# Conditioning products of the first layer: VectorE sums beside the projections, or one-column TensorE products between attention units

## The chip, the cores and the metric

The kernel runs on one NeuronCore of a Trainium2 chip. The metric is the device time of one execution in microseconds (us); the kernel before takes 2411.71 us, the median of three runs (2411.21 to 2413.84).

## The reference

A two-layer encoder on one sequence of 1024 tokens with 1024 features. Each layer has a token mixer and a gated feed-forward network, and both are steered by a conditioning vector c. What the change touches is the first line of the loop, for layer 0:

```python
cond = jax.nn.silu(c)
for i in range(DEPTH):
    mod = (cond @ ada_w[i] + ada_b[i])[:, None, :]        # 1024 x 6144 matrix per layer
    sh1, sc1, g1, sh2, sc2, g2 = jnp.split(mod, 6, axis=-1)   # chunks 0 to 5
    h = rmsnorm(x, norm_mix[i]) * (1 + sc1) + sh1
    y = windowed_gqa(...) if i % 2 == 0 else dilated_attention(...)
    x = x + g1 * y
    h = rmsnorm(x, norm_ffn[i]) * (1 + sc2) + sh2
    x = x + g2 * swiglu(h, ffn_w_in[i], ffn_w_out[i])
return rmsnorm(x, final_norm)
```

The product `cond @ ada_w[i]` is a vector times a matrix: six chunks of 1024 columns, 4 MB of weights each. Chunks 2 to 5 of layer 0 are the gate of its attention, the shift and scale of its feed-forward network, and that network's gate. Layer 0 has windowed attention with 16 query heads and 4 key heads over 8 blocks of 128 queries.

## The kernel before

Activations lie feature-major: 8 groups of 128 features on the partitions, 1024 tokens in two halves of 512 along the free dimension. A projection is a sum over 8 groups; since each float32 operand is split into a high and a low fp32r part, one step of it is three TensorE matmuls (L284, L285, L286 in `acc3`). Weights come by DMA into `raw`, ScalarE writes the high part (L180) and GpSimd the low part (L181).

`start` normalises the first token half and runs six projections; `layer_a` then runs, in its block around `pre_w`, four query tiles, the value tiles (`v_tile`, 256 columns, weights `wv`) and the key tiles of the second half. Beside these it makes chunks 2, 3 and 4 of the conditioning: `ada_steps` loads 128x1024 pieces of the matrix (L148) and adds each, times its element of `cond`, into `ada_acc` on VectorE (L151 for the first, L153 for the other seven); `ada_end` sums `ada_acc` over partitions by eight one-column products with a column of ones (L167), adds the bias (L169) and, for the scale chunk, makes the gain. `step` issues two such steps after each projection tile, held back by `issue_after`.

Then come the 32 attention units: for one key head and one query block, `first` makes the scores of four query heads (L490, L491), VectorE adds the bias and takes the minimum (L493), ScalarE the exponential (L503), VectorE scales (L510); `second`, two units later, transposes the probabilities on TensorE (L532), splits them (L534 on ScalarE, L535 on VectorE) and multiplies by the values (L526). `weave` interleaves the two with projection steps of the list `fill` (query tiles of the second half, then the output projection of the first half, then the first feed-forward tile). Those take PSUM banks from `bank`, two of them (tag `d`) during the units.

Chunk 5 is made by the same VectorE steps, issued at the end of `layer_a` (the last line before `return EARLY_A`), and the six chunks of layer 1 follow during the feed-forward network of layer 0 (`self.bg`). There the sum over partitions takes a VectorE transpose and reduction (L124, L126) and four small matmuls (L131).

The Tile framework orders each engine's instructions by its own model of their times with the order of the program as priority; the order is fixed when the kernel is built, and each engine works through its queue in that order. All DMAs are issued from SP's queue.

Of the kernel before, what the change touches and what calls it, by code (L numbers as in the profile page):

```python
# [7 lines left out]
F = mybir.dt.float32  # L8
# [3 lines left out]
ALU = mybir.AluOpType  # L12
AX = mybir.AxisListType

P = 128
D = 1024
KT = D // P
T = 1024
HT = 512
# [10 lines left out]
V_NM, V_NF, V_FN, V_C, V_AB = 0, 16, 32, 40, 48  # L30
# [1 line left out]
N_FIRST = 6  # L32
ADA_LATE = 1
BIAS_DVE = 5
PRE_PE = True
PRE_BUFS = 4, 1
PRE = (2,) * 14
PRE_LAG = 4
N_DVE = 5
A_BUFS = 2  # L40
RAW1 = 3
# [29 lines left out]
def run(steps):  # L71
    for _ in steps:
        pass


class Trunk:
    def __init__(self, ctx, tc, a, out, layers=(0, 1)):
        self.tc, self.nc, self.a, self.out, self.layers = tc, tc.nc, a, out, layers
        self.ctx = ctx
        self.t2, self.sq = 3, ("t2", 3)  # L80
        self.plan, self.ready = deque(), deque()
        self.ada_pe = False

    def sb(self, name):
        return self.tc.tile_pool(name=name, bufs=1, reuse_waits="tile")
# [49 lines left out]
    def ada_gain(self, layer, j, k0, k1):  # L135
        off = (V_NF if j else V_NM) + 8 * layer
        self.nc.vector.scalar_tensor_tensor(self.gain[:, layer, j, k0:k1], self.mod[:, layer, 24 * j + 8 + k0:24 * j + 8 + k1], 1.0,
                                            self.vec[:, off + k0:off + k1], op0=ALU.add, op1=ALU.mult)

    def ada_steps(self, layer, chunks, pool, bufs=2, abufs=1):  # L140

        nc = self.nc
        rest = iter(())
        for c in chunks:
            acc = pool.tile([P, D], F, name="ada_acc", tag="ada_acc", bufs=abufs)
            for k in range(KT):
                w = pool.tile([P, D], F, name="ada_w", tag="ada_w", bufs=bufs)
                nc.sync.dma_start(w, self.a["ada_w"][layer, k * P:(k + 1) * P, c * D:(c + 1) * D])  # L148
                s = self.cond[:, k:k + 1]
                if k == 0:  # L150
                    nc.vector.tensor_scalar(acc, w, s, None, op0=ALU.mult)  # L151
                else:
                    nc.vector.scalar_tensor_tensor(acc, w, s, acc, op0=ALU.mult, op1=ALU.add)  # L153
                if k == ADA_LATE:
                    run(rest)
                yield
            rest = self.ada_end(layer, c, acc, pool, bufs)
            next(rest)
            yield
        run(rest)  # L160

    def ada_end(self, layer, c, acc, pool, bufs):
        if self.ada_pe:
            yield
            ps = self.norm_bank()
            for j in range(KT):
                self.nc.tensor.matmul(ps[:, j:j + 1], lhsT=acc[:, j * P:(j + 1) * P], rhs=self.ones[:, 0:1], start=True, stop=True)  # L167
            cols = slice(8 * c, 8 * c + 8)
            self.nc.vector.tensor_tensor(self.mod[:, layer, cols], ps[:, 0:KT], self.vec[:, V_AB + 48 * layer:V_AB + 48 * layer + 48][:, cols], op=ALU.add)  # L169
            if c in (1, 4):  # L170
                self.ada_gain(layer, c // 3, 0, KT)
            return
        tr = pool.tile([P, D], F, name="ada_t", tag="ada_w", bufs=bufs)
        yield from self.ada_columns(layer, acc, tr, pool, slice(8 * c, 8 * c + 8))
        if c in (1, 4):
            self.ada_gain(layer, c // 3, 0, KT)
# [528 lines left out]
    def layer_a(self, h, x_src):  # L705
        nc, a, sb = self.nc, self.a, self.sb
        self.t2, self.sq = 4, ("t2", 4)
        layer = 0
# [22 lines left out]
            yield from self.project_steps(ps, self.weight("a_w_q", p, g), h[t])  # L731
            self.q_out_a(p, g, t, ps)

        with self.raw2_es, sb("pre_w") as prew, sb("pre") as pre:
            self.norm_bank = lambda: psp.tile([P, HT], F, name="ps_n", tag="o", bufs=2)
            self.banks += [(psp, tag, 2) for tag in BANKS_A]
            bg = self.ada_steps(0, (2, 3, 4), pre, *PRE_BUFS)
            self.ada_pe = PRE_PE
            w = prew.tile([P, 3, KT, 256], R, name="wv")[:, 0:2]

            todo = deque(PRE)

            done = []

            def step():
                done.append(self.evac)
                with ExitStack() as s:
                    if len(done) > PRE_LAG:
                        s.enter_context(self.tc.issue_after(done[-1 - PRE_LAG]))
                    for _ in range(todo.popleft()):  # L750
                        next(bg, None)

            for g in range(4):
                if 2 + 4 + g >= N_FIRST:
                    run(q_tile(1, g, 0))
                    step()
            for i in range(2):
                self.load_w(a["a_w_v"][i], w[:, :, 4 * i:4 * i + 4].rearrange("p s k f -> p s (k f)"))
            for tb in range(4):
                v_tile([w], tb)  # L760
                step()
            for tb in range(4, 8):
                v_tile([w], tb)
                step()
            for j in range(2):
                k_tile(j, 1)
                step()
            run(bg)
        self.ada_pe = False
        self.banks = deque([(self.psn, "d", 2)])  # L770
        self.norm_bank = self.bank
        wp, wk = (es.enter_context(sb(n)) for n in ("probs_a", "work_a"))
# [40 lines left out]
        oTs = []  # L813
        self.fill_start([q_tile(p, g, 1) for p in range(2) for g in range(4)] + [out_0(d) for d in range(KT)] + [self.up_early(layer, spill)], FILL_A, LOOK_A, 64)
        units = [(t, hd, b) for t in range(2) for hd in range(4) for b in range(4 * t, 4 * t + 4)]
        pend = deque()
        for i, (t, hd, b) in enumerate(units):
            if i % 16 == 0:
                oTs.append([[self.htile([4, HT]) for _ in range(2)] for _ in range(2)])
            if i == 18:  # L820
                self.most = 1000
            if i in (16, 24):
                self.fill_until(32 * (i // 8 - 1))
            if b % 4 == 0:
                bias = self.bias_tiles(wp, dist, SLOPE_A[4 * hd:4 * hd + 4], 6, nc.vector if i < BIAS_DVE else None)
            pt = self.weave(i, first(hd, b, bias), second(*pend.popleft()) if len(pend) > 1 else None)
            pend.append((hd, b, pt, oTs[t]))
        while self.fill:
            self.fill_step()
        while pend:  # L830
# [18 lines left out]
        self.hf[1] = self.norm_half(self.xs[1], ssq, layer, 1, self.pool, lows=LOWS["a_half1"])  # L849
        for f in range(1, EARLY_A):  # L850
            self.up(f, (0,))
        run(self.ada_steps(0, (5,), self.paux))
        return EARLY_A


# [428 lines left out]
def _arrays(np, i):  # L1284

    c = np.ascontiguousarray

    def cols(w, idx):

        w = w[:, idx]  # L1290
        return c(w.reshape(KT, P, -1, P).transpose(2, 1, 0, 3)).reshape(-1, P, D)

    def per_part(v):
        return v.reshape(-1, P).T

    o = {}
    o["x"] = c(i["x"][0].T).reshape(KT, P, T)
    o["vec"] = c(np.concatenate([per_part(i["norm_mix"]), per_part(i["norm_ffn"]), per_part(i["final_norm"]),
                                 per_part(i["c"]), per_part(i["ada_b"])], axis=1))
    o["sink"] = c(i["a_sink"])  # L1300
    o["cst"], o["dist"] = _constants(np)
    o["ada_w"] = c(i["ada_w"])
    w = i["ada_w"][0][:, :2 * D].reshape(KT, P, 2, KT, P)
    for d0, n in FIRST_D:
        o[f"ada_w0_{d0}"] = c(w[:, :, :, d0:d0 + n].transpose(1, 0, 2, 3, 4)).reshape(P, 2 * D * n)
    w = i["ffn_w_in"].reshape(2, KT, P, 2, NF, P)
    o["ffn_w_in"] = c(w.transpose(0, 4, 3, 2, 1, 5)).reshape(2, NF, 2, P, D)
    o["ffn_w_out"] = c(i["ffn_w_out"])
    w = i["a_w_in"][0]
    e = np.arange(64)  # L1310
    pair = [np.concatenate([((2 * p + par) * 4 + g) * 64 + e for par in range(2)]) for p in range(2) for g in range(4)]
    o["a_w_q"] = cols(w, np.concatenate(pair)).reshape(2, 4, P, D)
    o["a_w_k"] = cols(w, 1024 + np.arange(256))
    o["a_w_first"] = c(w[:, np.concatenate(pair[:2] + [1024 + np.arange(256)] + pair[2:N_FIRST - 2])]).reshape(KT, P, N_FIRST * P)
    o["a_w_v"] = c(w[:, 1280:].reshape(2, 4, P, 256).transpose(0, 2, 1, 3)).reshape(2, P, D)
    o["a_w_out"] = cols(i["a_w_out"][0][np.concatenate(pair)], np.arange(D))
    w = i["b_w_in"][0]
    o["b_w_q"] = cols(w, np.concatenate([gi * 512 + kv * 256 + g * 64 + e for gi in range(3) for g in range(4) for kv in range(2)])).reshape(3, 4, P, D)
    o["b_w_k"] = cols(w, 1536 + np.arange(384))
    o["b_w_v"] = c(w[:, 1920:].reshape(4, 2, P, 384).transpose(0, 2, 1, 3)).reshape(4, P, 768)  # L1320
    rows = np.concatenate([kv * 256 + g * 64 + e for g in range(4) for kv in range(2)])
    w = i["b_w_out"][0][rows].reshape(4, P, 4, 2, P)
    o["b_w_out"] = c(w.transpose(2, 1, 3, 0, 4)).reshape(4, P, D)
    return o
# [20 lines left out]
```

## Time and profile before

| | |
|---|---|
| median of the runs | 2411.71 us |
| profiled execution | 2411.33 us |
| its span, first to last instruction | 2409.5 us |
| TensorE busy | 2256.8 us, 94% |
| VectorE busy | 1282.8 us, 53% |
| ScalarE busy | 881.3 us, 37% |
| GpSimd busy | 751.4 us, 31% |
| DMA | 248.83 MB, 103 GB/s mean |

Busy time is the union of the instructions' recorded spans. The ends of matmuls are modelled, so a busy TensorE isn't one at its peak; the distance from one start to the next tells what a matmul takes. Where a matmul is float32 by float32, as L167, L226 and L532 are, what the trace records is passes: the 24 products of L167 stand as 48 records. The granted clock is a share of 2.4 GHz.

### The profile page before, as it was taken

Reading aid. Unit: us, or ns where it says so; the run is one execution under the profiler, and the core shown is the slowest. Engines: PE = TensorE matmul, PEld = TensorE weight load, DVE = VectorE, ACT = ScalarE, POOL = GpSimd, SP = SyncE. Lnnn points to the kernel's source line nnn. Section 1 sums busy time; section 2 is a strip of 40 time slices with the busy share of each in tenths; the row PEclk is TensorE's granted clock in tenths of the full one; section 3 lists DMA queues with packets and bytes.
Section 4 is the critical chain, followed back from the end, with each engine's and each line's share of the span. In section 5 each row is a group of like instructions: output and inputs, shape, how many; then the busy total and the mean of one; then the engine's idle time right before and its main releaser. Section 6 shows DMA issues by size and latency. Waiting matters only on the chain.

```text
span 2409.5 us, 28051 instructions
## 1 busy us (share of the span) xinstructions
PE 2256.8 (94%) x10484; PEld 1863.5 (77%) x10484; DVE 1282.8 (53%) x2265; ACT 881.3 (37%) x1749; POOL 751.4 (31%) x483
## 2 busy tenths in 40 slices
PE   6799898988999999999989999797999999999997
PEld 5687676767788888888879878576788888888886
DVE  8869999578533333333362577786633332222325
ACT  4549887332111111111242788673411111111111
POOL 4525453453122122222233344344431212222210
PEclk9899998999999999999999999898999999999998
DMA  7441123666411111111234765736321111111101
GB/s 281 150 144 36 40 84 132 214 205 219 158 60 39 50 44 53 44 53 44 79 121 155 197 189 179 212 89 202 96 70 53 51 46 53 53 53 44 53 18 70
DMA packets 131224, 248.83 MB, mean 103 GB/s; under 512 B 39312, under 2 KB 66576, under 8 KB 130064
## 3 DMA queue, kind: packets, MB, share of 16 engines
q1 hardware_dynamic: 131088, 247.05, 32.1%
q8 instruction: 82, 1.34, 0.2%
q14 instruction: 54, 0.44, 0.1%
HBM read 214.20 MB, written 30.70 MB: 102 GB/s over the span
## 4 chain that ended last, share of the span: by engine, by line
PE 71%; DVE 16%; DMA 6%; issue 3%; ACT 3%; POOL 1%; SPq 1%; DVEq 0%; ACTq 0%; POOLq 0%
PE ps_d L284 22%; PE ps_d L285 22%; PE ps_d L286 22%; DMA ada_w<-in_ada_w 3%; DVE ada_acc L153 3%; DVE p L493 2%; DVE pp L535 2%; PE ps_o L526 1%; PE ps_t L532 1%; DVE ht L256 1%; DVE p L510 1%; DVE h L262 1%; DMA ml_all<-sd 1%; PE ps_s L491 1%; PE ps_s L490 1%
## 5 line engine op out<-in xcount | busy, mean ns | idle before, releaser
L284 PE MATMUL ps_d<-h,w 128*128 128x512 f32 x1968 | 780.8, 399 | 22.4 <-ACT w L180 11.1
L285 PE MATMUL ps_d<-h,w 128*128 128x512 f32 x1968 | 779.2, 396 | 11.4 <-DVE h L262 9.9
L286 PE MATMUL ps_d<-h,w 128*128 128x512 f32 x1968 | 775.9, 395 | 3.8 <-POOL w L181 3.8
L181 POOL TENSOR_TENSOR w<-raw,w 128x1024 fp32r<-128x1024 f32 (+1 forms) x178 | 431.2, 2424 | 758.7 <-ACT w L180 745.9
L284 PEld LDWEIGHTS ps_d<-h,w 128*128 128x128 f32 x1968 | 374.8, 191 | 96.3 <-ACT w L180 13.7
L285 PEld LDWEIGHTS ps_d<-h,w 128*128 128x128 f32 x1968 | 376.6, 191 | 84.3 <-DVE h L262 12.8
L286 PEld LDWEIGHTS ps_d<-h,w 128*128 128x128 f32 x1968 | 375.3, 191 | 84.7 <-POOL w L181 5.8
L401 DVE TENSOR_TENSOR u<-silu,ps_d 128x512 f32<-128x512 f32 x88 | 60.4, 686 | 607.6 <-PE ps_d L286 591.1
L354 DVE SCALAR_TENSOR_TENSOR x<-ps_d,mod,x 128x512 f32<-128x512 f32 x368 | 270.3, 747 | 149.2 <-PE ps_d L286 149.2
L180 ACT ACTIVATE w<-raw 128x1024 fp32r<-128x1024 f32 (+1 forms) x178 | 185.6, 1046 | 361.2 <-PE ps_d L286 295.3
L284 PE MATMUL ps_d<-act,wo 128*128 128x512 f32 x704 | 275.4, 391 | 8.9 <-DVE x L354 4.8
L286 PE MATMUL ps_d<-act,wo 128*128 128x512 f32 x704 | 274.3, 390 | 0.0
L285 PE MATMUL ps_d<-act,wo 128*128 128x512 f32 x704 | 274.2, 390 | 0.0
L181 POOL TENSOR_TENSOR wo<-raw,wo 128x1024 fp32r<-128x1024 f32 x44 | 105.6, 2399 | 432.7 <-ACT wo L180 425.3
L180 ACT ACTIVATE wo<-raw 128x1024 fp32r<-128x1024 f32 x44 | 46.7, 1060 | 382.8 <-PE ps_d L286 340.2
L284 PEld LDWEIGHTS ps_d<-act,wo 128*128 128x128 f32 x704 | 132.2, 188 | 39.0 <-DVE x L354 6.6
L286 PEld LDWEIGHTS ps_d<-act,wo 128*128 128x128 f32 x704 | 132.2, 188 | 27.5
L285 PEld LDWEIGHTS ps_d<-act,wo 128*128 128x128 f32 x704 | 132.3, 188 | 26.9
L403 DVE TENSOR_TENSOR act<-u,act 128x512 fp32r<-128x512 f32 x88 | 124.8, 1418 | 47.3 <-ACT act L402 47.1
L153 DVE SCALAR_TENSOR_TENSOR ada_acc<-ada_w,cond,ada_acc 128x1024 f32<-128x1024 f32 x70 | 117.2, 1674 | 49.0 <-DMA ada_w<-in_ada_w 48.3
L402 ACT ACTIVATE act<-u 128x512 fp32r<-128x512 f32 x88 | 55.0, 625 | 218.2 <-DVE u L401 218.1
L490 PE MATMUL ps_s<-kh,q 128*128 128x384 f32 (+3 forms) x320 | 104.0, 329 | 21.5 <-DVE stat L493 11.6
(168 smaller groups left out, 2656.3 us busy)
## 6 DMA issues: line engine op xcount, KB each, us to landing
raw<-in_ffn_w_in SPq DMA_DIRECT2D x102, 512.0 KB
ada_w<-in_ada_w SPq DMA_DIRECT2D x80, 512.0 KB
raw<-in_ffn_w_out SPq DMA_DIRECT2D x44, 512.0 KB
raw<-in_b_w_q SPq DMA_DIRECT2D x24, 512.0 KB
qd<-qo SPq DMA_DIRECT2D x48, 256.0 KB
h<-in_ada_w SPq DMA_DIRECT2D x8, 1024.0 KB
raw<-in_a_w_out SPq DMA_DIRECT2D x16, 512.0 KB
q<-qd SPq DMA_DIRECT2D x16, 512.0 KB
```

What stands on the lines that cost most here:

```text
L153: nc.vector.scalar_tensor_tensor(acc, w, s, acc, op0=ALU.mult, op1=ALU.add)
L180: self.nc.scalar.activation(w[:, 0], raw, AF.Copy)
L181: self.nc.gpsimd.tensor_tensor(w[:, 1], raw, f32(w[:, 0]), op=ALU.subtract)
L284: mm(ps, lhsT=w[0], rhs=x[0], start=first, stop=False)
L285: mm(ps, lhsT=w[0], rhs=x[1], start=False, stop=False)
L286: mm(ps, lhsT=w[1], rhs=x[0], start=False, stop=last)
L354: self.nc.vector.scalar_tensor_tensor(x, ps, self.mod[:, layer, c * 8 + d:c * 8 + d + 1], x, op0=ALU.mult, op1=ALU.add)
L401: nc.vector.tensor_tensor(u, s, up, op=ALU.mult)
L402: nc.scalar.activation(act[:, 0, halves(t)], u, AF.Copy)
L403: nc.vector.tensor_tensor(act[:, 1, halves(t)], u, f32(act[:, 0, halves(t)]), op=ALU.subtract)
L490: nc.tensor.matmul(ps[:, lo:hi], lhsT=qs[g], rhs=kh, start=True, stop=False)
L493: nc.vector.tensor_tensor_reduce(pt[g][:, lo:hi], ps[:, lo:hi], bias[g][:, lo:hi], -1.0, -NEG if sink is None else sink[1][:, g:g + 1], op ...
```

## The change

Chunks 2 to 5 of layer 0 leave VectorE. A new generator, `ada_blocks`, takes the matrix in blocks of 1024 rows by 128 columns from a second copy of the weights in block order; for each block it issues eight products on TensorE with a 128x128 piece of the matrix as the stationary operand and one column of `cond` as the moving one, summed in PSUM. Two blocks go into one PSUM bank from `bank`; then VectorE adds the bias, and for chunks 1 and 4 it makes the gain. The weights come in pieces of 128x512 through three buffers. One step of the generator (two blocks: four loads, 16 products, one addition) is issued after each attention unit until the 16 steps are used up. The steps beside the projections, their pool and chunk 5's VectorE steps before the feed-forward network are gone.

```diff
-PRE_PE = True
-PRE_BUFS = 4, 1
-PRE = (2,) * 14
-PRE_LAG = 4
...
+    def ada_blocks(self, layer, chunks, pool, bufs):
+        nc = self.nc
+        bias = self.vec[:, V_AB + 48 * layer:V_AB + 48 * layer + 48]
+        for j0 in [8 * c + e for c in chunks for e in range(0, 8, 2)]:
+            ps = self.bank()
+            for j in range(2):
+                for k in range(KT):
+                    if k % 4 == 0:
+                        w = pool.tile([P, HT], F, name="ada_w", tag="ada_w", bufs=bufs)
+                        nc.sync.dma_start(w, self.a["ada_blocks"][layer, j0 + j][:, k * P:(k + 4) * P])
+                    nc.tensor.matmul(ps[:, j:j + 1], lhsT=w[:, k % 4 * P:k % 4 * P + P], rhs=self.cond[:, k:k + 1], start=k == 0, stop=k == KT - 1)
+            cols = slice(j0, j0 + 2)
+            nc.vector.tensor_tensor(self.mod[:, layer, cols], ps[:, 0:2], bias[:, cols], op=ALU.add)
+            if j0 // 8 in (1, 4):
+                self.ada_gain(layer, j0 // 24, j0 % 8, j0 % 8 + 2)
+            yield
...
-        with self.raw2_es, sb("pre_w") as prew, sb("pre") as pre:
+        with self.raw2_es, sb("pre_w") as prew:
...
-            bg = self.ada_steps(0, (2, 3, 4), pre, *PRE_BUFS)
-            self.ada_pe = PRE_PE
...
             for tb in range(4):
                 v_tile([w], tb)
-                step()
...
+        ada = self.ada_blocks(0, (2, 3, 4, 5), es.enter_context(sb("ada_a")), 3)
         pend = deque()
         for i, (t, hd, b) in enumerate(units):
...
             pend.append((hd, b, pt, oTs[t]))
+            next(ada, None)
...
-        run(self.ada_steps(0, (5,), self.paux))
         return EARLY_A
```

## Rows read from the trace of the kernel before

**Rows 1.** Stretches: us, busy by engine (instructions), granted clock, DMA share, GB/s

```profile
116.00:163.00 47.00, 41.35 (x263) 38.97 (x263) 31.33 (x37) 12.01 (x22) 13.49 (x6) 0.87 0.50 173
172.00:305.00 133.00, 120.31 (x630) 97.02 (x629) 128.73 (x332) 118.55 (x286) 59.83 (x41) 0.99 0.11 35
305.00:430.00 125.00, 114.06 (x569) 92.65 (x567) 113.97 (x264) 96.91 (x220) 49.63 (x43) 0.95 0.31 104
430.00:660.00 230.00, 206.15 (x900) 164.25 (x900) 158.87 (x150) 56.96 (x75) 91.07 (x49) 0.98 0.62 206
```

**Rows 2.** TensorE's waits, 55 to 172 us: who waits for whom, us, times, longest

```profile
PE ps_n L226 <- DVE ssq L219: 6.6, 1, 6.6
PE ps_d L284 <- DVE q L555: 2.6, 2, 1.3
...
PE ps_d L284 <- DVE vt L727: 4.1, 1, 4.1
```

**Rows 3.** Timeline, VectorE: start, us, line, operation, tiles, count, [idle before]

```profile
69.93 0.75 DVE L151 TENSOR_SCALAR ada_acc<-ada_w,cond 128x1024 f32<-128x1024 f32 x1
...
74.17 1.28 DVE L153 SCALAR_TENSOR_TENSOR ada_acc<-ada_w,cond,ada_acc 128x1024 f32<-128x1024 f32 x1
...
117.10 13.88 DVE L153 SCALAR_TENSOR_TENSOR ada_acc<-ada_w,cond,ada_acc 128x1024 f32<-128x1024 f32 x6
```

**Rows 4.** Timeline of TensorE: one-column products, and the matmul behind them

```profile
112.65 3.55 PE L167 MATMUL ps_n<-ones,ada_acc 128*128 128x1 f32 x16 [4.13 <-DVE ht L256]
116.06 0.56 PE L490 MATMUL ps_s<-kh,q 128*128 128x256 f32 x1
...
162.90 1.84 PE L167 MATMUL ps_n<-ones,ada_acc 128*128 128x1 f32 x16
164.60 0.37 PE L490 MATMUL ps_s<-kh,q 128*128 128x256 f32 x1
```

**Rows 5.** Groups of TensorE, 172 to 305 us: count | busy, mean ns | idle before

```profile
L526 PE MATMUL ps_o<-pp,vt 128*128 128x512 f32 x94 | 37.0, 429 | 8.2 <-DVE pp L535 7.7 <-ACT pp L534 0.3
L532 PE MATMUL ps_t<-cst,p 128*128 128x128 f32 x196 | 29.9, 273 | 0.7 <-DVE p L510 0.7
L286 PE MATMUL ps_d<-h,w 128*128 128x512 f32 x66 | 26.6, 404 | 0.0
...
L490 PE MATMUL ps_s<-kh,q 128*128 128x384 f32 x56 | 21.6, 386 | 2.8 <-DVE ml L493 2.7
```

**Rows 6.** Timeline of TensorE inside a unit

```profile
230.12 0.34 PE L491 MATMUL ps_s<-kl,q 128*128 128x384 f32 x1
230.29 0.39 PE L284 MATMUL ps_d<-h,w 128*128 128x512 f32 x1
230.52 0.40 PE L285 MATMUL ps_d<-h,w 128*128 128x512 f32 x1
...
231.23 0.60 PE L532 MATMUL ps_t<-cst,p 128*128 128x128 f32 x4
231.58 0.42 PE L490 MATMUL ps_s<-kh,q 128*128 128x384 f32 x1
231.84 0.33 PE L491 MATMUL ps_s<-kl,q 128*128 128x384 f32 x1
```

**Rows 7.** Chain that ended last, one load: start, us, what

```profile
162.63 3.27 DMA raw<-in_a_w_q
```

**Rows 8.** Timeline of TensorE around a wait in the units

```profile
245.83 0.50 PE L526 MATMUL ps_o<-pp,vt 128*128 128x512 f32 x1 [2.61 <-DVE pp L535]
...
248.34 0.63 PE L284 MATMUL ps_d<-h,w 128*128 128x512 f32 x1
248.77 0.63 PE L285 MATMUL ps_d<-h,w 128*128 128x512 f32 x1
```

**Rows 9.** Groups of VectorE, 445 to 475 us, chunk 5

```profile
L153 DVE SCALAR_TENSOR_TENSOR ada_acc<-ada_w,cond,ada_acc 128x1024 f32<-128x1024 f32 x7 | 14.7, 2105 | 3.8 <-DMA ada_w<-in_ada_w 3.8
```

**Rows 10.** SP queue's and TensorE's waits, 430 to 640 and 480 to 540 us

```profile
SPq L148 <- DVE ada_acc L153: 70.1, 38, 3.8
...
PE ps_d L226 <- DVE ssq L219: 5.8, 1, 5.8
```

More of the change, by code (lines that the diff above doesn't have):

```diff
@@ L81, in __init__ @@
         self.plan, self.ready = deque(), deque()
-        self.ada_pe = False
     def sb(self, name):
@@ L162, in ada_end @@
     def ada_end(self, layer, c, acc, pool, bufs):
[L163 to L172, printed above, removed]
         tr = pool.tile([P, D], F, name="ada_t", tag="ada_w", bufs=bufs)
@@ L732, in q_tile @@
             self.q_out_a(p, g, t, ps)
-        with self.raw2_es, sb("pre_w") as prew, sb("pre") as pre:
+        with self.raw2_es, sb("pre_w") as prew:
             self.norm_bank = lambda: psp.tile([P, HT], F, name="ps_n", tag="o", bufs=2)
             self.banks += [(psp, tag, 2) for tag in BANKS_A]
-            bg = self.ada_steps(0, (2, 3, 4), pre, *PRE_BUFS)
-            self.ada_pe = PRE_PE
             w = prew.tile([P, 3, KT, 256], R, name="wv")[:, 0:2]
[L741 to L751, printed above, removed]
             for g in range(4):
@@ L760, in layer_a @@
                 v_tile([w], tb)
-                step()
             for tb in range(4, 8):
                 v_tile([w], tb)
-                step()
             for j in range(2):
                 k_tile(j, 1)
-                step()
-            run(bg)
-        self.ada_pe = False
         self.banks = deque([(self.psn, "d", 2)])
@@ L1302, in _arrays @@
     o["ada_w"] = c(i["ada_w"])
+    o["ada_blocks"] = c(i["ada_w"].reshape(2, KT, P, 48, P).transpose(0, 3, 2, 1, 4)).reshape(2, 48, P, D)
     w = i["ada_w"][0][:, :2 * D].reshape(KT, P, 2, KT, P)
```

## The prediction

> **What bounds the kernel now.** I read the table of stretches first [rows 1], because the busy shares of the whole span mix stages with different limits. From 172 to 305 us, some 17 of the 32 attention units, VectorE is busy 128.7 of 133 us (97%); TensorE is busy 120.3, so it idles 12.7 us. In the second half of the units (305 to 430) VectorE is busy 114 of 125 and TensorE idles 11. The stretch ahead of the units, 116 to 163, has another limit: TensorE idles 5.7 of 47 us at a mean granted clock of 0.87 while VectorE is busy 31. There I read the waits: two long ones of TensorE are on VectorE's results, 6.6 us for the sum of squares and 4.1 us for a value tile, and two shorter ones, 2.6 us together, on query tiles [rows 2]. VectorE's timeline shows why: the six sums of one chunk stand in a row for 13.88 us right ahead of that value tile, and two single ones (0.75 and 1.28 us) among the sums of squares [rows 3]. From 430 to 660 us VectorE makes chunk 5 and layer 1's chunks; TensorE is busy 206 of 230 us, so it idles 24.
>
> So the change takes VectorE work from stages that wait for VectorE, and brings TensorE work into units in which VectorE is the fuller engine by 8 us in 133 but TensorE is nearly full too. The question is how much room TensorE has there.
>
> **What a one-column product costs.** The new products have the form of L167: a 128x128 float32 stationary operand and one float32 column. L167's 24 products stand as 48 records, two for each. Sixteen records take 162.90 to 164.60 us, 1.70 us to the start of the next matmul: 0.106 us each, 0.21 us a product, at the full clock; the same sixteen took 3.41 us (0.213 each) at 112.65, behind a 4.13 us wait, at the half clock [rows 4]. A 512-column matmul takes 0.23 us start to start [rows 6], so a product with one column is by no means free beside it. The Trainium skill, "TensorE: Matmul & The Clock Gate", puts the gap between matmuls of 1 to 64 columns at the issue floor of about 25 ns (section "Back-to-back issue gap"); the same page puts a weight load at its columns over 1.2 GHz, about 107 ns for 128 (section "LDWEIGHTS"). The rows agree with the load, not with the gap: one new stationary operand for each record.
>
> The change issues 4 chunks x 8 blocks x 8 pieces = 256 products, 512 records: 512 x 0.106 = **54 us** of TensorE, all in the first 16 units (3.4 us in each).
>
> **What room the units have.** The smaller figure for the room is the recorded idle time, 12.7 us [rows 1], most of it waits for VectorE: 7.7 us for the split probabilities, 2.7 us for score banks [rows 5]. The larger comes from counting starts: 94 + 196 matmuls of 512 columns (L284 and L285 stand 65 times each beside the 66 of L286) x 0.23 = 66.7; 112 score matmuls of 384 columns and the 32 records that remain of the 630, taken alike, 144 x 0.17 = 24.5; 196 transposes x 0.35/4 = 17.2 [rows 1, 5, 6]. The sum is 108.4, so 24.6 us would be free if every matmul followed the next at its best distance. It doesn't: the first score matmul behind the transposes took 0.26 us instead of 0.17 [rows 6]. I take 12 us, near the recorded idle time, since such losses come with each change of shape and the new products add changes: 54 - 12 = 42 us longer.
>
> **What else the products add in the units.** Sixteen additions and four gains on VectorE, small, no longer the bound there: nothing, and some 4 us if it stayed the bound. Each step takes one of the two `d` banks; a query tile of `fill` holds the other over more than two units, so a new query tile can wait for the bias addition, and the addition stands in VectorE's queue. Loads: 64 of 256 KB through three buffers. A step needs four; the fourth can start when the first buffer is read, 0.85 us into the block, and the first three are used up after 2.5 us. A 512 KB load in light traffic took 3.27 us [rows 7]; if half the bytes take 1.6 to 3.3, the wait is 0 to 1.6 us in each unit, 0 to 26 us in all, none if other matmuls stand between in TensorE's queue. Behind a waiting product stands all of TensorE's work, and behind a waiting load in SP's queue the query weights. The planner places the products by its own estimate of the load, so I take 5 us for banks and loads together. The units: **+47**, bounds +29 (54 - 25) and +80 (54 + 26).
>
> **What goes ahead of the units.** By position: the sums among the squares, 2.0 us [rows 3], and the waits behind sums of the two query tiles, 2.6 us [rows 2], that TensorE stands still for; the value tile's wait, 4.1 us; the other 32 records of L167, 32 x 0.106 = 3.4. Behind the 4.1 us wait a stretch at the half clock: around the wait at 245.83 us the same kind of drop has 512-column matmuls 0.43 us apart instead of 0.23 [rows 6, 8]; for some eight matmuls, my estimate of such a stretch, that is about 1.5. That is 13.6. The first sixteen records, 3.4 us at the half clock behind a 4.1 us wait [rows 4], cover a time in which the value weights are still being split, so most of that comes back as a wait for them; I take 2.4 of it. **-16**, bounds -10 (the query tiles wait for ScalarE instead, and the half clock stays) and -25 (all of it goes and the first units start earlier, with `dist` no longer queued in SP behind loads of the chunks).
>
> **What goes before the feed-forward network.** Chunk 5's seven sums take 14.7 us of VectorE [rows 9]. But the six chunks of layer 1 queue right behind: their loads wait for a free buffer, 70 us in all [rows 10], so they move up by one chunk and the waits of TensorE mostly stay, among them 5.8 us for the sum of squares [rows 10]. What is saved is about a seventh of the 24 idle us: **-3**, bounds 0 and -10.
>
> **Sum.** 47 - 16 - 3 = +28 us on the profiled execution's 2411.33 us (span 2409.5 and 1.8 around it; it lies 0.4 under the median): **2439 us**, 1.2% slower.
>
> **The rivals.** (1) Packing. TensorE's gaps are filled to the distance between starts (+29), the stages before give all they can (-25, -10): -6, 2405 us, faster by 0.25%. It decides as soon as the units grow by less than the 19 us that the other stages give. For it: the waits in the units are short and many, which a queue of ready products fills well, and VectorE gets slack. Against it: 24.6 us of room is a count without a single lost start. Chance 0.13.
> (2) The clock. One-column products leave the array nearly idle, and a block of 32 records takes 3.4 us. TensorE's clock fell to 1.2 GHz behind waits of 4.13 and 2.61 us [rows 4, 8]. If each block is followed by one stretch at 1.2 GHz, 16 x 1.5 = 24 us more, 2463 us; if the blocks run at it themselves, 512 x (0.213 - 0.106) = 55 more than the forecast, 2494. Against it: sixteen records at 162.90 ran at the full clock amid dense matmuls, but that block was half as long. The same page of the Trainium skill, section "HAM oscillation", tells of a product loop with thin operands whose clock falls again and again while it waits for its loads; no run here shows it yet. Chance 0.12.
> (3) Loads. The fourth load of each unit is late every time: +21 beyond my 5, 2460 us. Chance 0.08.
> (4) The gap rule. If the page's 25 ns held, the products would take 13 us, all inside the room: 2411 - 19 = 2392 us. Rows 4 speak against it four to one. Chance 0.03.
> (5) The change draws: the units grow by 15 to 24 us. Chance 0.06.
>
> **How the numbers follow.** My forecast, the units growing by some 30 to 65 us, has 0.58. Slower by over 0.2%, about what a measurement of this kernel can tell from no change: 0.58 + 0.12 + 0.08 = 0.78. Faster: 0.13 + 0.03 = 0.16. Same: 0.06. The range goes from the packing case, 2405, to past the load case and the milder clock case, 2472; outside it lie the gap rule, the harder clock case and sums of two misfortunes, about 0.2.
>
> **What would show it.** In the profile after: 512 records of one-column products about 0.106 us apart; units 0 to 15 over some 165 to 180 us instead of about 125, with VectorE's busy share down from 97% to some 75% and TensorE's idle time near zero; no 4 us wait for a value tile, and the units beginning 10 to 25 us earlier; the stretch behind the units shorter by a few us. The forecast is wrong if products stand closer than 0.1 us, if the granted clock in the units falls well under 0.95, or if the units still run at VectorE's pace.

## The result

The changed kernel takes 2470.11 us (median of four runs, 2467.45 to 2472.91) against 2412.20 us; the ratio is 1.024, with a 95% interval from 1.0222 to 1.0257. It is slower by 58 us where 27 were forecast. The profiled execution took 2472.41 us with a span of 2470.6, so 61.1 us more than the span before.

To see where, I take the first score matmul of a unit (L490 before, L494 after: four in each unit) as a milestone. Units are counted from 0; the very first is left out, since some of its scores run far ahead. All 128 of these records (32 units x 4) stand in every trace, so a milestone is found by counting. Each kernel was profiled once, and the runs of the kernel before range from 2405 to 2419 us on one chip: a stretch that differs by 2 or 3 us says little.

| first score of unit | before | after | difference |
|---|---|---|---|
| 1 | 166.0 us | 161.0 us | -5.0 |
| 17 | 280.0 | 345.2 | +65.2 |
| 31 | 393.6 | 454.6 | +61.0 |
| end of the span | 2409.5 | 2470.6 | +61.1 |

So the sixteen units with products grew by 70.2 us, from 114.0 to 184.2. The stages ahead gave 5.0 where 16 were forecast, the units without products 4.2, and everything behind the units nothing. Some 2.4 of those 4.2 us is work that only changed sides: 12 transposes and 6 products with the values stand before unit 17 in the changed kernel and behind it in the other. The stretches between the milestones, first of before and then of after (us, then busy time and instructions of TensorE, its weight loads, VectorE, ScalarE and GpSimd, then granted clock, DMA share, GB/s):

```profile
166.00:280.00 114.00, 103.94 (x542) 84.33 (x542) 109.17 (x291) 102.11 (x251) 52.64 (x37) 0.99 0.11 33
280.00:393.60 113.60, 107.26 (x555) 87.74 (x554) 109.59 (x267) 96.45 (x229) 50.97 (x34) 0.98 0.26 86
```

```profile
161.00:345.20 184.20, 183.93 (x1074) 167.12 (x1074) 119.25 (x321) 108.61 (x257) 52.23 (x37) 0.84 0.35 111
345.20:454.60 109.40, 103.87 (x537) 85.33 (x536) 105.52 (x256) 92.49 (x224) 51.52 (x33) 0.98 0.26 90
```

In the first line of after TensorE is busy 183.93 of 184.20 us: nothing of its queue waits. VectorE, the fuller engine before (109 of 114), is down to 119 of 184. But the granted clock is 0.84. A mean of 0.84 between the levels 1.0 and 0.5 is 32% of the stretch at 1.2 GHz, 59 us, in which half of the time is lost: some 29 us. The group of products, count, busy time, mean and idle time before, and TensorE's waits in that stretch:

```profile
L147 PE MATMUL ps_d<-cond,ada_w 128*128 128x1 f32 x512 | 65.5, 256 | 0.0
```

```profile
PE ps_t L536 <- DVE p L514: 0.3, 1, 0.3
```

That is the whole list of waits: one, of 0.3 us. The price of a record at each level, from the timeline of TensorE after (start, us, instruction):

```profile
219.12 2.73 PE L147 MATMUL ps_d<-cond,ada_w 128*128 128x1 f32 x24
221.72 0.42 PE L494 MATMUL ps_s<-kh,q 128*128 128x384 f32 x1
...
225.43 5.12 PE L147 MATMUL ps_d<-cond,ada_w 128*128 128x1 f32 x24
230.41 0.67 PE L494 MATMUL ps_s<-kh,q 128*128 128x384 f32 x1
```

The same two blocks as stretches, with the figures named above:

```profile
219.12:221.72 2.60, 2.60 (x26) 2.59 (x24) 0.84 (x2) 2.38 (x5) 0.73 (x1) 1.00 0.16 47
225.43:230.41 4.98, 4.98 (x25) 4.98 (x25) 2.53 (x7) 1.71 (x4) 1.27 (x1) 0.50 0.44 144
```

The first block of 24 takes 2.60 us at a granted clock of 1.00, 0.108 a record, as [rows 4] had it; the second takes 4.98 at 0.50, 0.208 a record, and the score matmul behind it is slow as well. The weight loads fill both blocks (2.59 of 2.60 and 4.98 of 4.98 us), one load for each record.

The start stage has a loss of its own. One load in SP's queue of before, then the queue of after and TensorE there (start, us, line, tile; in brackets what a matmul waited for):

```profile
43.35 0.45 SPq L628 DMA_DIRECT2D h<-in_ada_w  x1
```

```profile
9.69 3.20 SPq L146 DMA_DIRECT2D ada_w<-in_ada_blocks  x3
...
43.79 3.23 SPq L638 DMA_DIRECT2D raw<-in_a_w_first  x2
47.07 0.90 SPq L191 DMA_DIRECT2D raw<-in_a_w_q  x2
48.88 0.89 SPq L611 DMA_DIRECT2D xs<-in_x  x2
49.81 0.47 SPq L632 DMA_DIRECT2D h<-in_ada_w  x1
```

```profile
49.71 1.22 PE L288 MATMUL ps_d<-h,w 128*128 128x512 f32 x2 [1.66 <-ACT h L261]
...
117.42 0.55 PE L494 MATMUL ps_s<-kh,q 128*128 128x256 f32 x1 [9.70 <-DVE ht L260]
...
121.42 0.80 PE L288 MATMUL ps_d<-wv,h 128*128 128x256 f32 x2 [2.81 <-ACT wv L184]
```

The three buffers of the products' weights are free from the start of the kernel, so the planner put the first three loads at 9.7 us, among the weights of the start. What follows in the queue came out in another order too: the last piece of the start's own conditioning matrix (`h<-in_ada_w`) now stands behind `raw<-in_a_w_q` and `xs<-in_x`, which went out after it in the kernel before (50.92 and 51.96 us). It goes out at 49.81 us, where it went at 43.35. Behind the waits that follow, the granted clock is 0.50 from 50.7 to 58.8 us. The start's last projection ends at 79.6 us instead of 71.8.

### The profile page after: what moved, and what is told of

Same layout as the page of the kernel before. It is cut to its first block, busy times and chain, and to the rows that moved or that the text cites. A ratio compares the mean times of both kernels' runs of the same rounds, so it can differ in the third digit from the quotient of the medians.

```text
span 2470.6 us, 28976 instructions
## 1 busy us (share of the span) xinstructions
PE 2325.3 (94%) x10940; PEld 1935.3 (78%) x10940; DVE 1239.6 (50%) x2246; ACT 884.8 (36%) x1749; POOL 745.4 (30%) x483
## 4 chain that ended last, share of the span: by engine, by line
PE 76%; DVE 11%; DMA 6%; issue 3%; ACT 2%; POOL 1%; SPq 1%; DVEq 0%; POOLq 0%; ACTq 0%
PE ps_d L288 22%; PE ps_d L289 22%; PE ps_d L290 22%; DMA ada_w<-in_ada_w 3%; PE ps_d L147 2%; PE ps_o L530 2%; PE ps_t L536 2%; DVE ada_acc L167 2%; DVE p L497 1%; PE ps_s L494 1%; PE ps_s L495 1%; DVE ht L260 1%; DVE pp L539 1%; DMA ml_all<-sd 1%; DVE ssq L223 1%
## 5 line engine op out<-in xcount | busy, mean ns | idle before, releaser
L358 DVE SCALAR_TENSOR_TENSOR x<-ps_d,mod,x 128x512 f32<-128x512 f32 x368 | 270.6, 747 | 152.7 <-PE ps_d L290 151.0
L184 ACT ACTIVATE w<-raw 128x1024 fp32r<-128x1024 f32 (+1 forms) x178 | 185.6, 1046 | 368.2 <-PE ps_d L290 303.8
L494 PE MATMUL ps_s<-kh,q 128*128 128x384 f32 (+3 forms) x320 | 106.1, 335 | 33.3 <-DVE stat L497 16.5
L539 DVE TENSOR_TENSOR pp<-ps_t,pp 128x512 fp32r<-128x512 f32 x168 | 114.8, 687 | 24.8 <-ACT pp L538 22.6
```

The source lines that it names most:

```text
L184: self.nc.scalar.activation(w[:, 0], raw, AF.Copy)
L358: self.nc.vector.scalar_tensor_tensor(x, ps, self.mod[:, layer, c * 8 + d:c * 8 + d + 1], x, op0=ALU.mult, op1=ALU.add)
L494: nc.tensor.matmul(ps[:, lo:hi], lhsT=qs[g], rhs=kh, start=True, stop=False)
L539: nc.vector.tensor_tensor(pp[n, 1], tp[n], f32(pp[n, 0]), op=ALU.subtract)
```

## The experiments

Theory: the products cost TensorE what [rows 4] says, 54 us less its idle time; the rest is a clock that one-column products bring down, and loads that went ahead in SP's queue. Rivals: the loads or the banks stall the units; another order alone is to blame; a record costs the same wherever it stands. Times are medians, each beside the kernel before on the same chip (2412.7 and 2412.4 us).

**No products.** Chunks 2 to 5 of layer 0 are left out but for their bias.

```diff
-            ps = self.bank()
...
-                    nc.tensor.matmul(ps[:, j:j + 1], lhsT=w[...], rhs=self.cond[:, k:k + 1], ...)
-            nc.vector.tensor_tensor(self.mod[:, layer, cols], ps[:, 0:2], bias[:, cols], op=ALU.add)
+            nc.vector.tensor_copy(self.mod[:, layer, cols], bias[:, cols])
```

> The 256 products, their loads and the banks they take are left out; chunks 2 to 5 of layer 0 are the bias alone. Theory (the products and the clock that they bring down are the whole loss): units 1 to 17 back at VectorE's pace, about 114 us instead of 184, and what is left is the gain of the stages ahead and of the feed-forward network, 2412 - 16 - 3 = some 2393 us by the prediction's figures, some 2404 if the stages ahead give only the 5 us that the changed kernel's trace shows. Rival (something else in the new order costs, for instance the order of the loads in SP's queue at the start): 2415 us or more, with the start stage still 8 us late.

2389.04 us, ratio 0.9899 (0.9878 to 0.9919). Units 1 to 17 take 115.9 us, the clock is 1.00 there, and unit 1 begins at 151.4 us:

```profile
151.40:267.30 115.90, 104.83 (x543) 83.00 (x543) 112.11 (x291) 102.52 (x252) 53.78 (x37) 1.00 0.12 37
```

The products with their loads cost 81 us of the changed kernel; the VectorE sums cost at most 24 of the kernel before. The stages ahead could give 14.6 us, near the 16 forecast; of them the changed kernel has only 5.0. Of the 24 us some 10 lie behind the units, where the planner's order came out differently; since the changed kernel leaves out chunk 5's sums as well and gains nothing there, that part is hardly the sums' own (see the sixth experiment).

**Loads held.** One edit: the products' loads are issued behind the last load of the start stage.

```diff
+                        with self.tc.issue_after(self.loaded):
-                        nc.sync.dma_start(w, self.a["ada_blocks"]...)
+                            nc.sync.dma_start(w, self.a["ada_blocks"]...)
```

> The only edit: every load of a product's piece is issued behind the last load of the start stage, so that the first three no longer stand among the weights of the start. Theory (those three loads reordered SP's queue and cost the start stage its 8 us): the last start projection ends near 72 us instead of 79.6, total 2470 - 8 = 2462 us. Rival (the start stage is late for another reason, or what it gives back ends in the wait for the value weights behind it): 2468 to 2471 us.

2458.07 us, ratio 1.0192 (1.0165 to 1.0219). SP's queue there, then TensorE's last matmul of the start and the first score of unit 0, and units 1 to 17:

```profile
43.61 0.42 SPq L633 DMA_DIRECT2D h<-in_ada_w  x1
...
53.34 1.76 SPq L147 DMA_DIRECT2D ada_w<-in_ada_blocks  x3
```

```profile
71.65 0.39 PE L291 MATMUL ps<-h,w 128*128 128x512 f32 x1
...
107.52 0.55 PE L495 MATMUL ps_s<-kh,q 128*128 128x256 f32 x1 [5.66 <-DVE ht L261]
```

```profile
151.00:336.60 185.60, 183.81 (x1062) 166.47 (x1061) 119.63 (x323) 108.12 (x259) 52.02 (x37) 0.83 0.35 110
```

The matrix piece goes out at 43.61 again, the start ends at 72.0, 7.6 us earlier, and unit 1 begins at 151.0 instead of 161.0: the order of the loads cost the changed kernel 10.0 us ahead of the units, since the wait ahead of unit 0's first scores is shorter too (5.66 us instead of 9.70). Units 1 to 17 take 185.6, 1.4 more. The total moved by 12, 13.9 in the profiled executions, because the part behind the units is 5.9 us shorter as well, in another order. The clock in the units stays low (0.83), so this loss and the clock's are separate.

**64 columns.** Every product streams the conditioning column 64 times; the weight loads, the records and their number stay.

```diff
-nc.tensor.matmul(ps[:, j:j + 1], lhsT=w[...], rhs=self.cond[:, k:k + 1], ...)
+nc.tensor.matmul(ps[:, 64 * j:64 * j + 64], lhsT=w[...], rhs=self.cond[:, k:k + 1].broadcast_to([P, 64]), ...)
...
-ps[:, 0:2]
+ps[:, 0:65:64]
```

> Each product gets the same conditioning column 64 times as its moving operand, so the array works on 64 columns a record instead of one; the sum of the columns' starts is unchanged if the weight load sets the distance. Theory (the clock falls because one-column products leave the array idle): granted clock in the units near 0.97 instead of 0.84, units 1 to 17 some 155 to 160 us instead of 184, total 2441 to 2447 us. Rival (the clock falls for the weight loads or the breaks between kinds of matmul, or 64 columns cost time of their own): clock still near 0.84, 2470 us or more.

2443.52 us, ratio 1.0128 (1.0104 to 1.0152). Units 1 to 17, and a block of records:

```profile
161.80:316.40 154.60, 154.03 (x1050) 140.75 (x1050) 120.23 (x316) 107.82 (x255) 53.09 (x38) 1.00 0.41 132
```

```profile
208.07 2.79 PE L147 MATMUL ps_d<-cond,ada_w 128*128 128x64 f32 x24
210.66 0.42 PE L494 MATMUL ps_s<-kh,q 128*128 128x384 f32 x1
```

24 records take 2.59 us, 0.108 each as with one column, and the clock is 1.00 in the whole stretch. It shrinks from 184.2 to 154.6 us, by the 29 to 30 that the clock of 0.84 had cost; over all 30 units from 1 to 31, which hold the same other matmuls in both kernels, it is 266.2 us against 293.6, 27.3 less. More work for the array made the kernel 27 us faster. The planner's order of TensorE changed a little as well; that this isn't the cause is borne out by the held loads (another order, one column, 0.83) and by the two spread runs below (one column 0.97, 64 columns 1.00). TensorE is still busy 154.0 of 154.6 us: what is left, 40.6 us over the 114.0 before, is 54 less 13.

**Spread.** Eight products after each of 32 units instead of sixteen after each of 16: a `yield` after each block.

> The same 256 products, but eight of them (16 records, 1.7 us) after each of the 32 units instead of sixteen after each of the first 16. Theory (long blocks of products bring the clock down, and the first half's idle time is used up): the second half's idle time of some 11 us serves too and shorter blocks leave the clock up, 2470 - 11 - 15 to 25 = 2434 to 2444 us. Rival (each record costs the same wherever it stands, clock included): only the idle time, 2459 us.

2430.52 us, ratio 1.0069 (1.0045 to 1.0094).

```profile
160.80:295.60 134.80, 132.27 (x830) 118.71 (x830) 115.66 (x305) 106.21 (x254) 53.13 (x37) 0.97 0.31 100
295.60:427.70 132.10, 127.91 (x764) 112.04 (x762) 108.98 (x279) 96.34 (x228) 50.00 (x34) 0.97 0.39 124
```

The 30 units take 266.9 us against 293.6, so 27 us less, with one column still: the clock holds at 0.97 when the products come in shorter runs among other matmuls (mostly 2 to 10 records in a row, where the changed kernel has 8 to 24). The edit also halves the products in each unit; which of the two keeps the clock up wasn't separated. The other 14 us lie behind the units (another order there). "Each record costs the same wherever it stands" is refuted.

**All three.** Held loads, 64 columns, spread.

> The three edits together: first loads behind the start stage, 64 columns, eight products after each of the 32 units. Theory (the losses are the start's 12 us, the clock's 29 us, and what is left is 54 us of TensorE less its idle time in the units): units begin at 153 us as in the run with held loads, the 31 units take 228 + 54 - 18 to 25 = 257 to 264 us at a clock near 1, total 2412 - 13 + 29 to 36 = 2428 to 2435 us, some 10 less if the planner's order of layer 1 comes out as in the spread run (2430). So still slower than before: the work itself is too much for TensorE. Rival (the clock and the start explain it all and one-column products are nearly free): 2400 us or less.

2422.44 us, ratio 1.0039 (1.0026 to 1.0051).

```profile
151.90:285.50 133.60, 130.95 (x838) 116.94 (x837) 116.96 (x306) 106.37 (x255) 53.99 (x38) 1.00 0.34 103
285.50:414.30 128.80, 124.90 (x755) 108.71 (x755) 112.57 (x279) 96.07 (x228) 50.10 (x33) 1.00 0.41 128
```

The clock is 1.00, the start is on time (unit 1 begins at 151.9; the 153 expected is the third score matmul of unit 1 with held loads), and the 30 units still take 262.4 us, 35 more than before. With clock and start taken out, 54 us of products find some 19 us of room, of which some 2.5 is 11 projection matmuls that moved behind the last unit. The last unit begins 21 us later than before; only a part behind the units that is 12 us shorter, in another order, brings the total within 10. The products as such lose here.

**Sums later.** The kernel before with its VectorE sums behind the query tiles.

```diff
-PRE = (2,) * 14
-PRE_LAG = 4
+PRE = (0,) * 4 + (2,) * 8 + (4,) * 2
+PRE_LAG = 1
```

> The kernel before with its VectorE sums of chunks 2 to 4 moved: none beside the four query tiles, two or four after each value and key tile, each behind the tile before (PRE and PRE_LAG alone). Theory (before the units TensorE waits for VectorE only where a run of sums stands ahead of a tile's evacuation): the waits behind the sums among the query tiles go (some 5 us) and the value tile's 4.1 us too, total 2412 - 5 to 10 = 2402 to 2407 us. Rival (the sums only move the wait, since 29 us of them and 12 MB of loads must fit into some 45 us): 2410 to 2416 us.

2403.22 us, ratio 0.9962 (0.9947 to 0.9976): faster than both kernels, and in the range forecast, but not for the reason forecast. TensorE at the value tiles, and units 1 to 17:

```profile
113.85 0.79 PE L284 MATMUL ps_d<-wv,h 128*128 128x256 f32 x2 [10.21 <-ACT wv L180]
...
124.42 0.39 PE L284 MATMUL ps_d<-wv,h 128*128 128x256 f32 x1 [0.86 <-DVE vt L727]
```

```profile
158.70:282.50 123.80, 110.29 (x557) 89.19 (x558) 117.92 (x299) 102.70 (x251) 53.28 (x36) 0.94 0.14 47
```

The 4.1 us wait of [rows 2] is down to 0.9 and unit 1 begins 7.3 us earlier, so ahead of the units the theory holds. But the sums now reach into the units, which take 123.8 instead of 114.0. The last unit begins at 396.1, 2.5 us later than before, and the first feed-forward product on VectorE stands at 431.62 us instead of 429.27. All of the gain comes later: from the last unit to the end 2005.0 us against 2015.9. Most of it arises in layer 1, which the edit doesn't touch, between some 1570 and 1670 us. TensorE's longest wait there, before (1610 to 1665 us) and in this run (1612 to 1662; total, times, longest):

```profile
PE ps_d L284 <- ACT w L180: 8.9, 1, 8.9
```

```profile
PE ps_d L284 <- ACT w L180: 5.0, 3, 3.5
```

So up to the last unit the rival (the wait moves) holds, and the gain belongs to a side effect of planning. The other runs bear that out, though none tests it alone: where ScalarE's order behind unit 31 is nearly that of before, the part from there to the end takes 2012 to 2018 us (the changed kernel, 64 columns, the last run below), and where it differs, 2001 to 2010 (no products, held loads, spread, all three, and this run).

**One chunk as products.** Chunk 4 alone as 64 products of 64 columns, eight after every third unit, with held loads; chunks 2 and 3 as VectorE sums two by two behind the query tiles (PRE = 0 x 4, 2 x 10, PRE_LAG = 1); chunk 5 as before.

> The kernel before with chunk 4 alone as products (64 of them, 64 columns, held loads, eight after every third unit), chunks 2 and 3 as VectorE sums behind the query tiles, chunk 5 as before. Theory (TensorE's idle time in the units takes about 13 to 18 us of products for nothing, and the stages ahead give back a part of their waits): units +0 to 5 us, the stages ahead -6 to -12, total 2402 to 2410 us. Rival (products cost their full 13.6 us wherever they stand): 2412 to 2420 us.

2408.73 us, ratio 0.9985 (0.9975 to 0.9995): a gain of 0.15%. Units 1 to 17:

```profile
157.50:277.60 120.10, 112.94 (x638) 95.03 (x638) 111.35 (x296) 101.72 (x251) 53.54 (x37) 0.99 0.19 58
```

Unit 1 begins 8.5 us earlier than before, and units 1 to 17 take 6.1 more; unit 31 begins at 389.7, 3.9 earlier. All 64 products stand in the 30 units from 1 to 31, 13.8 us by the record, and these take 4.6 us more: two thirds of the products' time found room, one third didn't. The last VectorE sum of chunks 2 and 3 ends at 151.8 us, ahead of these units, so the sums of the run above have no part in it. The total and its two parts lie where the theory had them. Behind unit 31, in nearly the order of before, 2.5 us go again, too little for one profiled execution to settle.

## Why the prediction was right or wrong

**What bounds the kernel: right.** The units were near TensorE's capacity, and filled it once the products came (183.93 of 184.20 us).

**The price of a product: right.** 0.106 us a record forecast, 0.108 at the full clock, and the same with 64 columns. The weight loads fill the blocks, so they set it, as [rows 4] and not the gap rule of rival (4) had it.

**The room: right.** 54 - 12 = 42 us forecast; with the clock up and nothing else changed in intent it is 40.6. The count of starts (24.6 us of room) would have been wrong; spread over 32 units, all the room found was 19. But I had the stretches of [rows 1] wrong: 172 to 305 us holds some 19 units, not 17, and 305 to 430 goes past the last unit, which begins at 393.6. By the milestones TensorE idled 10.1 us in units 1 to 17 and 6.3 in units 17 to 31, not 12.7 and 11, so the 12 that I took came out near by some luck.

**Banks and loads, +5: wrong, nothing.** One wait of 0.3 us in the whole stretch, and none of it for a load or a bank.

**The clock: the step that failed.** It stood as a rival at 0.12 with 24 to 55 us and was left out of the sum; it cost 27 (30 units, against 64 columns) to 29 (by the mean clock). The evidence that I took against it, sixteen records at the full clock at 162.90 us [rows 4], was one short block amid dense matmuls, and I said so, but gave it more weight than it carries. The milder price, one stretch at 1.2 GHz for each unit (24 us), was nearly the size. The prediction's own sign of being wrong, a granted clock well under 0.95 in the units, came true at 0.84.

**The stages ahead, -16: the term was mis-sized by what I left out.** With the start on time the units begin 15.0 us earlier (held loads), 14.6 with no products, so the sum over the waits that VectorE's sums caused was sound. But of the loads I asked only how they'd behave in the units, not when the first of them could go out. The order of SP's queue at the start cost 10.0 us, 7.6 of it in the start stage; what was left is outside the bounds that I gave (-10 to -25; measured -5.0).

**Before the feed-forward network, -3: nothing.** The lower bound holds: layer 1's chunks move up, and TensorE waits 6.8 us for the sum of squares where [rows 10] had 5.8. The second half of the units gave 4.2 us that I hadn't forecast, 2.4 of them work that had only moved to the first.

Sum as forecast: +47 - 16 - 3 = +28. As measured in the profiled execution: +70.2 - 5.0 - 4.2 + 0.1 = +61.1.

## What to carry to other kernels

A small product has two prices on TensorE: the weight load that sets its distance to the next, and what a run of such products does to the clock of the matmuls around it. Count the first against the idle time that the stretch really has; for the second, look for a block as long as the one planned, and where there is none, carry the slow level in the sum. When loads get buffers that are free early, ask where the planner will put the first of them, and look behind the changed part too: an order that shifts there can move the time by more than the edit.

## What the runs showed of the hardware

The clock fell to 0.84 on average while TensorE's queue never waited: an engine busy by its records isn't enough to keep it at 2.4 GHz. The same records with 64 columns in place of one cost the same 0.108 us and kept the clock at 1.00; 27 us of the total came back for 64 times the arithmetic. A record's distance follows the clock even where weight loads set it: 0.108 us at a granted clock of 1.00, 0.208 at 0.50. The Trainium skill, "TensorE: Matmul & The Clock Gate", section "HAM oscillation", explains falling clocks by waits for loads between groups of products; here there were none, so the measured case is another one.
